# Two plain blocks in place of three at the start of channel mixers 2 to 4, with their gates behind the first seven-product block's products

## The chip, the cores and the metric

The kernel runs on one core of a Trainium2 chip, as one program. The time is the device's own time of one execution in microseconds (us); the median of several executions counts. TensorE is called PE, VectorE DVE, ScalarE ACT, GpSimd POOL and SyncE, which issues most of the DMAs, SP.

## The reference, cut to what matters

The program is a decoder trunk of two layers on 512 tokens of width 1024 in float32. Each layer has a channel mixer, a token mixer and a second channel mixer, and a last norm ends it. The change touches the channel mixers alone, of which there are four:

```python
def rmsnorm(x, g):
    y = x32 * lax.rsqrt(jnp.mean(x32 * x32, axis=-1, keepdims=True) + RMS_EPS)
    return y.astype(x.dtype) * g

def swiglu(x, w_gate, w_up, w_down):          # 1024 -> 2816 -> 1024
    return (jax.nn.silu(x @ w_gate) * (x @ w_up)) @ w_down

for i in range(2):
    h = h + 0.5 * swiglu(rmsnorm(h, ffn_norm_a[i]), ...)
    h = h + (mla_mixer, nsa_mixer)[i](...)
    h = h + 0.5 * swiglu(rmsnorm(h, ffn_norm_b[i]), ...)
return rmsnorm(h, final_norm)
```

## The kernel before, in words

The activations lie transposed, channels on the partitions and the 512 tokens along the free dimension, in eight tiles `h`. PE is given its operands as fp32r, and each operand is split into a high part (a copy by ACT) and a low part (the difference, by DVE), and each product is three matmuls: high by high, high by low, low by high. `split` does that; its two lines stand in the profile as L205 (ACT) and L206 (DVE). A weight slab is 128 x 1024 (all 1024 inputs of 128 outputs); `wslab` loads it by a DMA from SP and splits it (L176, L178).

`ffn(idx, ...)` is one channel mixer; `idx` 0 to 3 are mixers 1 to 4. Its 2816 hidden channels are 22 blocks `f` of 128. There are two kinds of block:

- A plain block multiplies a gate slab and an up slab by the activations (`plain`; tiles `pg` and `pu`, L401 to L403): 2 slabs x 8 inputs x 2 token halves x 3 = 96 matmuls of 256 columns.
- A seven-product block (`wsums` and `product`; tiles `px`, `pq`, `pg`, L386 to L388) computes the gate and up outputs of both token halves together, from sums of weights and sums of activations: 7 products x 4 inputs x 3 = 84 matmuls. DVE makes the weight sums (L372 to L376; `s1`, and in place in `rg` or `wr`, `ru`), ACT copies partial outputs out of PSUM (L543 to L550) and DVE adds the rest (L551, L553). The products come as 1, 7, 6, 2, 5, 4, 3. `w[1], w[2]` are halves of the slab's own split `w`; `w[7], w[4]` are `wh`/`wl` made from `ru`, `w[6], w[3]` those made from the sums in `rg` (or `wr`), `w[5]` those made from `s1`.

The activations' sums for these products are made by `combine(p)`, p = 0 to 3, once for each mixer: two scaled copies by ACT (`y`), three differences by DVE (`u`, L271 to L273), and a split of 1024 columns (`four`). A mixer therefore begins with plain blocks, `PLAIN = 3` of them, while the four combines are made; the other 19 are seven-product blocks.

The norm is applied late: `norm_col` finds 1/rms of each token (a chain of small DVE operations on `small`), `norm_bcast` spreads it by four PE transposes into a PSUM bank `pb`, and ACT copies it to a tile `row`. `gate(f, g)` multiplies the gate output by `row`, applies Silu (ACT, L434) and multiplies by `row` again (L433, L435); `act(f)` multiplies by the up output (L444, L446) and splits the result into `ah`, `al`. ACT must load its table of Silu once ahead of these where another function was used before; a one-element Silu on `tiny` (L513) sets its place.

The down projection runs in units: three blocks `f` (NG = 3) into one of eight output tiles, 9 matmuls of 512 columns (`pd`, L197 to L199), with a slab `wdr` from SP that is split into `wd`. The eight units of blocks 0 to 2 stand behind the seven-product blocks 3, 4 and 5, three, three and two of them. `settle` (the loop over `gates` on L525 to L527) lets ACT read one column of each plain gate bank, so that ACT is seen to be done with it.

A scheduler sets the order in each engine's queue from the program's text, its dependencies and a model of costs; each engine runs its queue in that order. `issue_after(x)` keeps an instruction behind x in that order. Two of them matter: the split of the slab of block `PLAIN + 1` is kept behind `evicted`, ACT's copy after product 5 of a block (here of block `PLAIN`), and the split of the down units of blocks 0 to 2 is kept behind the copy to `row` in mixers 2 and 4.

PSUM has eight banks in rings: `mm` 2, `S` 2, `T` 3, `o` 1. The gates of the plain blocks take all of `T`; the up outputs alternate between `mm` and `S`.

Of the kernel before, what the change touches and what calls it, by code (L numbers as in the profile page):

```python
# [11 lines left out]
F32 = mybir.dt.float32  # L12
F32R = mybir.dt.float32r
I32 = mybir.dt.int32
AF = mybir.ActivationFunctionType
# [33 lines left out]
PLAIN = 3  # L49
# [12 lines left out]
class Kern:  # L62
# [278 lines left out]
    def wsums(self, idx, f):  # L341
# [3 lines left out]
        if f == PLAIN:  # L345

            rg = fp.tile([P, 1024], F32, tag="fr", bufs=3, name="rg")
        else:
            rg = self.wp.tile([P, 1024], F32, tag="wr", bufs=2, name="wr")
# [6 lines left out]
        def split(src, pool, tag, bufs):  # L356
# [8 lines left out]
            with self.tc.issue_after(self.evicted.ins) if f == PLAIN + 1 else nullcontext():  # L365
                self.split(src, hi, lo)
# [57 lines left out]
    def ffn(self, idx, gain_next, ap, tp):  # L424
        nc, a = self.nc, self.a
        self.scr, self.fp = (tp, "sq", 1), tp
        ah, al, ht, row = {}, {}, [], None
        tg, tu, units = {}, {}, []
# [11 lines left out]
        def act(f):  # L440
            t = tu[f]
            if f < PLAIN:
                t = tu_tile()
                nc.vector.scalar_tensor_tensor(t, tu[f], -1.0, tg[f], op0=ALU.mult, op1=ALU.mult)  # L444
            else:
                nc.vector.tensor_tensor(t, t, tg[f], op=ALU.mult)  # L446
# [12 lines left out]
        def unit(tag, b0, c):  # L459
# [4 lines left out]
            with self.tc.issue_after(self.spread.ins) if idx % 2 and not b0 else nullcontext():  # L464
                self.split(raw.rearrange("p (k c) -> p k c", c=P), *w)
# [21 lines left out]
        gates = [self.bank("T", "pg") for _ in range(PLAIN)]  # L487
        for f, g in enumerate(gates):
# [23 lines left out]
            if f == 1:  # L512
                nc.scalar.activation(self.tiny[:, 4:5], col[:, 0:1], AF.Silu, scale=-1.0)  # L513
                pb = self.norm_bcast(col)
                row = tp.tile([P, S], F32, tag="row", bufs=1, name="row")
                self.spread = nc.scalar.activation(row, pb, AF.Copy)
                for e in range(2):
                    gate(e, gates[e])
                    act(e)
            elif f:  # L520
                gate(f, g)
                act(f)
            for p in (((0,), (1,), (2, 3)) if idx else ((0, 1), (2,), (3,)))[f]:
                self.combine(p)
        t = self.tiny  # L525
        for i, g in enumerate(gates[::-1]):
            nc.scalar.activation(t[:, i + 1 : i + 2], g[:, 0:1], AF.Identity, bias=t[:, i : i + 1])  # L527

        tail = PLAIN + (NF - 2 - PLAIN) // NG * NG
        for f in range(PLAIN, NF):  # L530
            if f % NG == 0 and f <= tail:
# [13 lines left out]
            nc.scalar.activation(uq[:, :HS], q, AF.Copy)  # L545
            self.product(6, w, x, False, False)
# [976 lines left out]
```

## Time and profile before

| | us |
|---|---|
| median of 3 runs | 1867.71 (1866.2 to 1868.5) |
| the profiled execution's own time | 1865.65 |
| its span, first to last instruction | 1863.9 |
| granted PE clock over the span | 0.999 |
| PE busy | 1849.9, 12448 matmuls |
| DVE, ACT, POOL busy | 1506.2, 1068.5, 297.4 |
| mixers 2, 3, 4: PE's first plain matmul | 546.45, 884.06, 1516.19 |

A row of the time line reads: start in us from the span's start, length in us, engine, line of the kernel, operation, output <- inputs, sizes, and, in brackets, how long the engine had been idle before it and what ended that. SPq is SP's queue of DMA issues. The lengths of PE's matmuls overlap, so their places are read from one start to the next.

### The profile page before, as it was taken

The numbers are of one execution on the slowest core, as the hardware profiler recorded it, in microseconds if no ns is written. First come the engines' busy times: TensorE is split into PE (matmuls) and PEld (weight loads), VectorE is DVE, ScalarE is ACT, GpSimd is POOL, SyncE is SP. The second block draws the span as 40 slices with busy tenths as digits, with TensorE's granted clock in tenths as the row PEclk, the third lists the DMA queues.
The fourth block names the chain that finished last, engine by engine and source line by source line (L and its number), as shares of the span: only waits on it lengthen the run. The fifth ranks groups of instructions, "written<-read, shape, count | busy, mean of one in ns | idle before, by whom it ended". The sixth has DMA issues, their size and how long they took to land.

```text
span 1863.9 us, 32992 instructions
## 1 busy us (share of the span) xinstructions
PE 1849.9 (99%) x12448; PEld 1686.5 (90%) x12448; DVE 1506.2 (81%) x2810; ACT 1068.5 (57%) x1997; POOL 297.4 (16%) x370
## 2 busy tenths in 40 slices
PE   9999999999999999999999999999999999999998
PEld 9999999878889999998999999988888889999997
DVE  8988886688779888886898887676878888888885
ACT  7555553577666555554655555445776865555554
POOL 0000000258830000001000000022666620000000
PEclk9999999999999999999999999999999999999999
DMA  6333331334433333322433332162433133333321
GB/s 238 125 114 102 102 91 47 117 103 105 115 124 112 116 102 104 112 74 64 142 120 110 107 107 80 44 180 84 108 109 103 41 118 122 114 104 105 104 78 69
DMA packets 84335, 196.38 MB, mean 105 GB/s; under 512 B 10944, under 2 KB 38464, under 8 KB 84176
## 3 DMA queue, kind: packets, MB, share of 16 engines
q1 hardware_dynamic: 81664, 191.34, 33.7%
q10 hardware_dynamic: 2512, 2.93, 0.5%
q8 instruction: 98, 1.61, 0.4%
q14 instruction: 61, 0.50, 0.1%
HBM read 178.44 MB, written 2.16 MB: 97 GB/s over the span
## 4 chain that ended last, share of the span: by engine, by line
PE 92%; DVE 3%; ACT 1%; issue 1%; POOL 1%; DMA 1%; SPq 0%; ACTq 0%; DVEq 0%; POOLq 0%
PE pd L198 8%; PE pd L197 8%; PE pd L199 8%; PE px L386 6%; PE px L388 5%; PE px L387 5%; PE pg L386 4%; PE pg L387 4%; PE pg L388 4%; PE pq L386 4%; PE pq L387 4%; PE pq L388 4%; PE o L1326 2%; PE pt L1299 2%; PE po L197 1%; PE po L199 1%
## 5 line engine op out<-in xcount | busy, mean ns | idle before, releaser
L198 PE MATMUL pd<-al,wd 128*128 128x512 f32 x576 | 225.1, 391 | 0.0
L197 PE MATMUL pd<-ah,wd 128*128 128x512 f32 x576 | 224.9, 390 | 0.0
L199 PE MATMUL pd<-ah,wd 128*128 128x512 f32 x576 | 224.6, 390 | 0.0
L289 POOL TENSOR_TENSOR s<-s,sq 128x512 f32<-128x512 f32 x38 | 54.9, 1445 | 1051.2 <-ACT sq L285 1051.2
L206 DVE TENSOR_TENSOR w<-wr,w 128x1024 fp32r<-128x1024 f32 x72 | 88.1, 1224 | 132.9 <-ACT w L205 132.6
L386 PE MATMUL px<-four,wh 128*128 128x256 f32 x608 | 168.4, 277 | 0.4 <-ACT pg L543 0.3
L388 PE MATMUL px<-four,wl 128*128 128x256 f32 x608 | 168.1, 277 | 0.2 <-DVE wl L206 0.2
L386 PE MATMUL pq<-four,wh 128*128 128x256 f32 x608 | 167.9, 276 | 0.0
L387 PE MATMUL px<-four,wh 128*128 128x256 f32 x608 | 167.9, 276 | 0.0
L388 PE MATMUL pq<-four,wl 128*128 128x256 f32 x608 | 167.8, 276 | 0.0
L387 PE MATMUL pq<-four,wh 128*128 128x256 f32 x608 | 167.8, 276 | 0.0
L457 DVE SCALAR_TENSOR_TENSOR h<-pd,h 128x512 f32<-128x512 f32 x216 | 147.5, 683 | 13.7 <-PE pd L199 13.6
L205 ACT ACTIVATE wd<-wdr 128x384 fp32r<-128x384 f32 x192 | 99.2, 519 | 98.5 <-ACT wd L205 58.2
L199 PEld LDWEIGHTS pd<-ah,wd 128*128 128x128 f32 x576 | 108.2, 188 | 22.7
L176 ACT ACTIVATE w<-wr 128x1024 fp32r<-128x1024 f32 (+3 forms) x89 | 80.8, 908 | 82.9 <-PE pd L199 19.2
L197 PEld LDWEIGHTS pd<-ah,wd 128*128 128x128 f32 x576 | 108.1, 188 | 20.5
L198 PEld LDWEIGHTS pd<-al,wd 128*128 128x128 f32 x576 | 108.1, 188 | 19.5
L178 DVE TENSOR_TENSOR w<-wr,w 128x1024 fp32r<-128x1024 f32 (+3 forms) x75 | 78.4, 1046 | 48.9 <-ACT w L176 48.7
L717 ACT ACTIVATE p<-p,small 128x512 f32<-128x512 f32 (+2 forms) x192 | 106.9, 558 | 19.1 <-DVE small L716 15.4
L386 PEld LDWEIGHTS px<-four,wh 128*128 128x128 f32 x608 | 114.1, 188 | 1.7 <-ACT pg L543 0.8
L388 PEld LDWEIGHTS px<-four,wl 128*128 128x128 f32 x608 | 114.1, 188 | 0.8 <-DVE wl L206 0.6
L386 PEld LDWEIGHTS pq<-four,wh 128*128 128x128 f32 x608 | 114.1, 188 | 0.4 <-ACT uq L545 0.4
(379 smaller groups left out, 6153.9 us busy)
## 6 DMA issues: line engine op xcount, KB each, us to landing
wr<-in_w_gu SPq DMA_DIRECT2D x93, 512.0 KB, 3.3
ru<-in_w_gu SPq DMA_DIRECT2D x76, 512.0 KB, 4.1
wdr<-in_w_down SPq DMA_DIRECT2D x192, 192.0 KB, 2.4
wr<-in_w_down SPq DMA_DIRECT2D x24, 256.0 KB, 2.6
wr<-in_mla_w_o SPq DMA_DIRECT2D x8, 512.0 KB, 3.6
th<-btab_d SPq DMA_DIRECT2D x16, 256.0 KB, 3.8
wr<-in_nsa_w_q SPq DMA_DIRECT2D x8, 512.0 KB, 3.9
wr<-in_nsa_w_o SPq DMA_DIRECT2D x8, 512.0 KB, 3.8
```

The source lines that it names most:

```text
L176: self.copied = nc.scalar.activation(wh[:, m], raw[:, m], AF.Copy)
L178: nc.vector.tensor_tensor(wl[:, m], raw[:, m], f32v(wh[:, m]), op=ALU.subtract)
L197: mm(out, wh, xh, start=first, stop=False)
L198: mm(out, wh, xl, start=False, stop=False)
L199: return mm(out, wl, xh, start=False, stop=last)
L205: nc.scalar.activation(hi, src, AF.Copy)
L206: (nc.gpsimd if pool else nc.vector).tensor_tensor(lo, src, f32v(hi), op=ALU.subtract)
L386: mm(out, wh[:, p], xh, start=first and p == 0, stop=False, skip_group_check=True)
L387: mm(out, wh[:, p], xl, start=False, stop=False, skip_group_check=True)
L388: mm(out, wl[:, p], xh, start=False, stop=last and p == KP - 1, skip_group_check=True)
L457: nc.vector.scalar_tensor_tensor(self.h[c], p, 0.5, self.h[c], op0=ALU.mult, op1=ALU.add)
L717: nc.scalar.activation(p_sb[:, :n], p_sb[:, :n], AF.Exp, bias=nm, scale=-1.0, accum_out=sm)
```

## The change

Mixer 1 keeps its three plain blocks. In mixers 2 to 4 block 2 becomes a seven-product block, the two plain blocks each make two combines ahead of it, and the copy to `row`, the gates and acts of blocks 0 and 1 and `settle` move behind products 1 and 7 of that block in the program's text. `PLAIN` becomes `self.plains`, 2 or 3. Block 2 has no down units behind it; those of blocks 0 to 2 stay behind blocks 3, 4 and 5, and their splits are kept behind `evicted` (of the block that they follow) in place of the copy to `row`. The split kept behind `evicted` is that of block 3, the second seven-product block.

```diff
@@ -46,7 +46,6 @@
 LASTK = 4
 HS = S // 2
 KP = KC // 2
-PLAIN = 3
 PAD = 16
 TILES = 24
 XC = P + 2
@@ -342,7 +341,7 @@
 
 
         nc, fp, w_gu = self.nc, self.fp, self.a["w_gu"]
-        if f == PLAIN:
+        if f == self.plains:
 
             rg = fp.tile([P, 1024], F32, tag="fr", bufs=3, name="rg")
         else:
@@ -362,7 +361,7 @@
             else:
                 hi = pool.tile([P, n], F32R, tag=tag[0], bufs=bufs, name="wh")
                 lo = pool.tile([P, n + 2 * PAD], F32R, tag=tag[1], bufs=bufs, name="wl")[:, 2 * PAD :]
-            with self.tc.issue_after(self.evicted.ins) if f == PLAIN + 1 else nullcontext():
+            with self.tc.issue_after(self.evicted.ins) if f == self.plains + 1 else nullcontext():
                 self.split(src, hi, lo)
             return [(hi[:, x : x + S].rearrange("p (k c) -> p k c", c=P), lo[:, x : x + S].rearrange("p (k c) -> p k c", c=P))
                     for x in range(0, n, S)]
@@ -425,6 +424,7 @@
         nc, a = self.nc, self.a
         self.scr, self.fp = (tp, "sq", 1), tp
         ah, al, ht, row = {}, {}, [], None
+        self.plains = 2 if idx else 3
         tg, tu, units = {}, {}, []
 
         def gate(f, g):
@@ -439,7 +439,7 @@
 
         def act(f):
             t = tu[f]
-            if f < PLAIN:
+            if f < self.plains:
                 t = tu_tile()
                 nc.vector.scalar_tensor_tensor(t, tu[f], -1.0, tg[f], op0=ALU.mult, op1=ALU.mult)
             else:
@@ -461,7 +461,7 @@
             w = [ap.tile([P, NG * P], F32R, tag=t, bufs=3, name="wd").rearrange("p (k c) -> p k c", c=P) for t in ("dh", "dl")]
             raw = ap.tile([P, NG * P], F32, tag="dr", bufs=2, name="wdr")
             nc.sync.dma_start(raw, a["w_down"][idx, c, :, b0 * P : (b0 + NG) * P])
-            with self.tc.issue_after(self.spread.ins) if idx % 2 and not b0 else nullcontext():
+            with self.tc.issue_after(self.evicted.ins) if idx and not b0 else nullcontext():
                 self.split(raw.rearrange("p (k c) -> p k c", c=P), *w)
             p = self.bank(tag, "pd")
             down(p, w, b0, b0 + NG)
@@ -484,7 +484,21 @@
             return self.norm_col(D, self.s2)
 
 
-        gates = [self.bank("T", "pg") for _ in range(PLAIN)]
+        def spread():
+            nonlocal row
+            pb = self.norm_bcast(col)
+            row = tp.tile([P, S], F32, tag="row", bufs=1, name="row")
+            nc.scalar.activation(row, pb, AF.Copy)
+            for e in range(2):
+                gate(e, gates[e])
+                act(e)
+
+        def settle():
+            t = self.tiny
+            for i, g in enumerate(gates[::-1]):
+                nc.scalar.activation(t[:, i + 1 : i + 2], g[:, 0:1], AF.Identity, bias=t[:, i : i + 1])
+
+        gates = [self.bank("T", "pg") for _ in range(self.plains)]
         for f, g in enumerate(gates):
             u = tu[f] = self.bank(("mm", "S")[f % 2], "pu")
             if idx == f == 0:
@@ -511,24 +525,19 @@
                 col = late()
             if f == 1:
                 nc.scalar.activation(self.tiny[:, 4:5], col[:, 0:1], AF.Silu, scale=-1.0)
-                pb = self.norm_bcast(col)
-                row = tp.tile([P, S], F32, tag="row", bufs=1, name="row")
-                self.spread = nc.scalar.activation(row, pb, AF.Copy)
-                for e in range(2):
-                    gate(e, gates[e])
-                    act(e)
-            elif f:
+            if f == 1 and idx == 0:
+                spread()
+            elif f > 1:
                 gate(f, g)
                 act(f)
-            for p in (((0,), (1,), (2, 3)) if idx else ((0, 1), (2,), (3,)))[f]:
+            for p in (((0, 1), (2, 3)) if idx else ((0, 1), (2,), (3,)))[f]:
                 self.combine(p)
-        t = self.tiny
-        for i, g in enumerate(gates[::-1]):
-            nc.scalar.activation(t[:, i + 1 : i + 2], g[:, 0:1], AF.Identity, bias=t[:, i : i + 1])
-
-        tail = PLAIN + (NF - 2 - PLAIN) // NG * NG
-        for f in range(PLAIN, NF):
-            if f % NG == 0 and f <= tail:
+        if idx == 0:
+            settle()
+
+        tail, left = (NF - 2) // NG * NG, 1
+        for f in range(self.plains, NF):
+            if f % NG == 0 and NG <= f <= tail:
                 units = [partial(unit, b0=f - NG, c=c) for c in range(KC)]
                 left = NG if f < tail else NF - tail
             n = -(-len(units) // left)
@@ -543,6 +552,9 @@
             nc.scalar.activation(g[:, :HS], x, AF.Copy)
             self.product(7, w, q, True, False)
             nc.scalar.activation(uq[:, :HS], q, AF.Copy)
+            if idx and f == self.plains:
+                spread()
+                settle()
             self.product(6, w, x, False, False)
             nc.scalar.activation(uq[:, HS:], x, AF.Copy)
             self.product(2, w, g[:, :HS], False, True)
```

What this does to the queues is shown at three places of mixer 2. In the names, the number tells tiles apart. Before, `rg_6834`, `w_6839`, `px_6858`, `pq_6859` belong to the first seven-product block (f = 3), `w_7018`, `px_7037`, `pq_7038` to the second (f = 4) and `w_7197` to the third. Now `rg_6686`, `px_6710`, `pq_6711` belong to the first (f = 2), `w_6848`, `px_6867`, `pq_6868` to the second (f = 3), and `w_7027`, `pq_7047` to the third (f = 4).

ACT, where the table load for Silu stands. Before:

```order
L176 ACTIVATE w_6697<-wr_6695 128x1024
L513 ACT_TABLE_LOAD
L513 ACTIVATE gains_77<-small_76 128x1
L176 ACTIVATE w_6750<-wr_6748 128x1024
L516 ACTIVATE row_6662<-pb_6657 128x512
```

Now:

```order
L204 ACTIVATE wh_6702<-rg_6686 128x1024
L527 ACT_TABLE_LOAD
L527 ACTIVATE gains_77<-small_76 128x1
L552 ACTIVATE pg_6712<-px_6710 128x256
L554 ACTIVATE uq_6713<-pq_6711 128x256
L491 ACTIVATE row_6746<-pb_6741 128x512
```

The load now stands between the split of the first seven-product block's weight sums and the copy of its product 1.

DVE, from the gates of blocks 0 and 1 on. Before:

```order
L433 TENSOR_TENSOR tg_6664<-pg_6406,row_6662 128x512
L433 TENSOR_TENSOR tg_6674<-pg_6407,row_6662 128x512
L206 TENSOR_TENSOR wd_6958<-wdr_6959,wd_6957 128x384
L435 TENSOR_TENSOR tg_6664<-tg_6664,row_6662 128x512
L435 TENSOR_TENSOR tg_6674<-tg_6674,row_6662 128x512
L444 SCALAR_TENSOR_TENSOR tu_6668<-pu_6409,tg_6664 128x512
L444 SCALAR_TENSOR_TENSOR tu_6678<-pu_6549,tg_6674 128x512
L433 TENSOR_TENSOR tg_6801<-pg_6408,row_6662 128x512
L206 TENSOR_TENSOR al_6671<-tu_6668,ah_6670 128x512
L206 TENSOR_TENSOR w_6839<-rg_6834,w_6839 128x1024
```

Now:

```order
L205 TENSOR_TENSOR wl_6703<-rg_6686,wh_6702 128x1024
L433 TENSOR_TENSOR tg_6748<-pg_6406,row_6746 128x512
L433 TENSOR_TENSOR tg_6758<-pg_6407,row_6746 128x512
L435 TENSOR_TENSOR tg_6748<-tg_6748,row_6746 128x512
L444 SCALAR_TENSOR_TENSOR tu_6752<-pu_6408,tg_6748 128x512
L435 TENSOR_TENSOR tg_6758<-tg_6758,row_6746 128x512
L205 TENSOR_TENSOR w_7027<-wr_7022,w_7027 128x1024
L205 TENSOR_TENSOR al_6755<-tu_6752,ah_6754 128x512
L444 SCALAR_TENSOR_TENSOR tu_6762<-pu_6558,tg_6758 128x512
L563 TENSOR_TENSOR tu_6714<-px_6710,uq_6713 128x256
L565 TENSOR_TENSOR tu_6714<-pq_6711,uq_6713 128x256
L205 TENSOR_TENSOR w_6848<-wr_6843,w_6848 128x1024
```

The gates stood ahead of the low half `w` of the first seven-product block; they now stand behind that block's low halves and ahead of the second block's, and the third block's `w_7027` stands ahead of the second's `w_6848`, as on ACT.

PE, where product 6 of the second seven-product block ends. Before:

```order
L386 MATMUL px_7037<-four_6828,wh_7029 128x256
L387 MATMUL px_7037<-four_6828,wh_7029 128x256
L388 MATMUL px_7037<-four_6828,wl_7030 128x256
L386 MATMUL pg_7039<-x_6263,w_7018 128x256
L387 MATMUL pg_7039<-x_6263,w_7018 128x256
```

Now:

```order
L385 MATMUL px_6867<-four_6683,wh_6859 128x256
L386 MATMUL px_6867<-four_6683,wh_6859 128x256
L387 MATMUL px_6867<-four_6683,wl_6860 128x256
L385 MATMUL pq_7047<-four_6545,wh_7032 128x256
L386 MATMUL pq_7047<-four_6545,wh_7032 128x256
L385 MATMUL px_6867<-four_6545,wh_6863 128x256
L386 MATMUL px_6867<-four_6545,wh_6863 128x256
```

Two matmuls of product 7 of the third block, whose weights `wh_7032` ACT makes from a sum on DVE, have moved ahead of product 5 of the second.

## The prediction

> **What bounds the kernel now.** I read the page first, then the busy time of each engine in stretches around the start of the second channel mixer, then the time line of each engine there.
>
> ```profile
> PE 1849.9 (99%) x12448; PEld 1686.5 (90%) x12448; DVE 1506.2 (81%) x2810; ACT 1068.5 (57%) x1997; POOL 297.4 (16%) x370
> PE 92%; DVE 3%; ACT 1%; issue 1%; POOL 1%; DMA 1%; SPq 0%; ACTq 0%; DVEq 0%; POOLq 0%
> ```
>
> PE carries 92% of the chain that ended last. A matmul taken away is worth its place in PE's row, as long as PE then finds its operands ready. The first and the last of the 48 matmuls of one slab of up-weights give that place:
>
> ```profile
> 551.94 0.28 PE L401 MATMUL pu<-x,w 128*128 128x256 f32 x1
> ...
> 557.27 0.28 PE L403 MATMUL pu<-x,w 128*128 128x256 f32 x1
> ```
>
> 47 steps in 5.33 us are 0.1134 us a matmul (the 0.28 us are its length; they overlap).
>
> The stretches below are of the second mixer: its first two plain blocks, the third, the first seven-product block, and the three down-projection units behind it. Columns: stretch, length, busy us of PE, weight loads, DVE, ACT, POOL, granted clock, DMA.
>
> ```profile
> 546.40:569.30 22.90, 22.90 (x200) 22.69 (x200) 21.45 (x37) 17.48 (x22) 3.29 (x2) 1.00 0.53 186
> 569.30:580.90 11.60, 11.55 (x102) 11.38 (x101) 10.29 (x18) 7.46 (x15) 0.00 (x0) 1.00 0.35 109
> 580.90:590.50 9.60, 9.60 (x84) 9.40 (x83) 6.70 (x10) 5.93 (x9) 0.00 (x0) 1.00 0.30 96
> 590.50:596.80 6.30, 6.30 (x31) 5.28 (x31) 6.30 (x11) 3.41 (x7) 0.00 (x0) 1.00 0.26 86
> ```
>
> This is where the argument turns. Over the kernel DVE is busy 81%, but in the two plain blocks 21.45 of 22.90 us, since the four sums for the seven products are made there. DVE is free for 1.45 + 1.31 + 2.90 = 5.66 us up to the end of the first seven-product block, and that is all the room.
>
> **What the change adds and removes.** Three mixers each turn one plain block (96 matmuls) into a seven-product one (84): 36 matmuls x 0.1134 = 4.1 us less on PE. DVE's prices, as starts from one row to the next:
>
> ```profile
> 555.19 1.22 DVE L206 TENSOR_TENSOR four<-u,four 128x1024 fp32r<-128x1024 f32 x1
> ...
> 558.40 0.42 DVE L273 TENSOR_TENSOR u<-y,u 128x256 f32<-128x256 f32 x1
> 558.74 0.42 DVE L272 TENSOR_TENSOR u<-y,u 128x256 f32<-128x256 f32 x1
> ...
> 561.14 0.15 DVE L294 TENSOR_SCALAR small<-pc 128x4 f32<-128x4 f32 x1
> 561.22 0.41 DVE L272 TENSOR_TENSOR u<-y,u 128x256 f32<-128x256 f32 x1
> ...
> 575.99 0.68 DVE L433 TENSOR_TENSOR tg<-pg,row 128x512 f32<-128x512 f32 x1
> 576.59 0.68 DVE L206 TENSOR_TENSOR al<-tu,ah 128x512 fp32r<-128x512 f32 x1
> 577.18 1.21 DVE L206 TENSOR_TENSOR w<-rg,w 128x1024 fp32r<-128x1024 f32 x1
> 578.32 0.68 DVE L206 TENSOR_TENSOR al<-tu,ah 128x512 fp32r<-128x512 f32 x1
> ...
> 588.11 1.23 DVE L206 TENSOR_TENSOR w<-wr,w 128x1024 fp32r<-128x1024 f32 x1 [2.83 <-ACT w L205]
> ```
>
> So 1.14 us for 1024 wide, 0.60 for 512, 0.34 for 256, some 0.08 to 0.10 for the norm's small ones; another engine sees a result 0.08 us after the next could start, and starts about 0.06 us later. A seven-product block costs DVE 3 x 1.14 + 0.60 (weights' low halves), 4 x 0.60 (weight sums), 2 x 0.34 (the outputs' sums), 4 x 0.60 (gate and act) = 9.5 us; a plain one 2 x 1.14 + 4 x 0.60 = 4.7. That is 4.8 us more for DVE, and 1.4 us less of PE to hide it, against 5.66 us of room: already 0.5 us short if nothing ever waits. The work that hid it is one plain block's PE time and the units behind the first seven-product block; now a second seven-product block follows the first with no units between.
>
> **First wait: product 6 of the new block, second mixer alone.** ACT must copy product 1 out of px before product 6 may add to it. In the order after, ACT's row ahead of that copy is: high half of rg, table load, the small Silu. Their prices:
>
> ```profile
> 566.66 1.05 ACT L176 ACTIVATE w<-wr 128x1024 fp32r<-128x1024 f32 x1
> 567.73 1.28 ACT L513 ACT_TABLE_LOAD   x1
> 569.53 0.20 ACT L513 ACTIVATE gains<-small 128x1 f32<-128x1 f32 x1 [0.52 <-DVE small L304]
> ...
> 570.77 0.60 ACT L516 ACTIVATE row<-pb 128x512 f32<-128x512 f32 x1
> ...
> 588.38 0.37 ACT L550 ACTIVATE pg<-px 128x256 f32<-128x256 f32 x1 [0.30 <-PE px L388]
> ```
>
> The table load stood beside a full PE before. The high half of rg needs the weight sums in rg, on DVE. From the row at 555.19 DVE has, up to that sum, 8 rows of 1.14, 5 of 0.60, 6 of 0.34 and 11 of 0.10 = 15.3, so 570.5. ACT then: 570.65 + 1.07 (from the row at 566.66 to the next) + 1.28 + 0.20 + a copy of 0.37 = 573.6. On PE's side:
>
> ```profile
> 569.32 0.28 PE L403 MATMUL pu<-x,w 128*128 128x256 f32 x1
> 569.65 0.62 PE L323 MATMUL pb<-ident,small 128*128 128x128 f32 x4
> 570.02 0.37 PE L401 MATMUL pg<-x,w 128*128 128x256 f32 x1
> ```
>
> PE ends the second plain block at 569.4, needs 24 x 0.1134 for products 1 and 7 and 0.37 + 0.11 for the transposes: 572.6. A wait of 1.0. In the third mixer the order has no table load there, in the fourth it stands earlier; between 0 and the second's 1.0 I take 0.2 and 0, nearest to "no load in the way".
>
> **Second wait: the second seven-product block.** DVE starts on the two moved gates when the norm's row is spread: 573.6 + 0.37 (copy of pq) + 0.60 = 574.5, 0.9 after product 6 began. From there to the sum that product 7 of the *third* seven-product block needs, DVE's order has 17 rows of 0.60, 4 of 1.14 and 2 of 0.34 = 15.4, and three short waits for ACT (Silu, the high half of w, 0.4 together): 590.3. With 0.14 to get there ACT splits that sum in 1.07, so PE may take the two matmuls on pq_7047 at 591.6. PE itself has between its product 6 at 573.6 and these two 120 matmuls (five products of the first block; 1, 2, 7, 4 and 6 of the second) = 13.6 us: it would be there at 587.2. The difference, 4.4 us, is PE's wait. It comes in pieces, by the same count up to each row: about 0.9 at the third matmul of product 1 (ACT may split w_6848 only behind its copy after product 5, and ahead of it ACT and DVE split a later block's w_7027; behind it on ACT stand wh_6853 for product 7 and the high half of act 1), 0.9 at product 2 (ACT's copy of px stands behind a Silu that waits for DVE), 0.75 at product 6, 1.1 at pq_7047, the rest small. In-order PE makes each of them whole: behind pq_7047 stands product 5, which is ready. Four shorter ones follow, up to the end of the third seven-product block (product 3, the low half of the first wd, product 6, the third unit), 0.05 to 0.1 each with 0.11 for the restart (next fence): 0.7. So 5.1 a mixer, 15.3 for three. The relation of row, gates and product 6 is the same in mixers 3 and 4, and so is the order from there on.
>
> The bounds of this term: at least 0.5 (the balance above, if every row were at its best place); at most DVE's 4.8 us and the whole 2.83 us idle of the row at 588.11 lost as well, 7.6.
>
> **What goes away.** Four waits of PE around the old first seven-product block:
>
> ```profile
> 583.86 0.28 PE L387 MATMUL px<-four,wh 128*128 128x256 f32 x1
> 584.13 0.39 PE L388 MATMUL px<-four,wl 128*128 128x256 f32 x1
> 584.36 0.28 PE L386 MATMUL px<-four,wh 128*128 128x256 f32 x1
> ...
> 615.42 0.28 PE L388 MATMUL pq<-four,wl 128*128 128x256 f32 x1
> 615.98 0.39 PE L386 MATMUL px<-four,wh 128*128 128x256 f32 x1 [0.28 <-ACT pg L543]
> ...
> 920.74 0.28 PE L388 MATMUL pq<-four,wl 128*128 128x256 f32 x1
> 921.12 0.38 PE L386 MATMUL px<-four,wh 128*128 128x256 f32 x1
> ...
> 1553.43 0.28 PE L387 MATMUL px<-four,wh 128*128 128x256 f32 x1
> 1553.94 0.39 PE L388 MATMUL px<-four,wl 128*128 128x256 f32 x1 [0.24 <-DVE wl L206]
> ```
>
> After a wait the next step is 0.23, as from 584.13 to 584.36, so each costs 0.11 beyond its own step less 0.1134: 0.27 + 0.56 + 0.37 + 0.51 = 1.7 us. I take all of it as gone, since the places are worked through anew above.
>
> **At nothing:** the third combine brought forward lies within DVE's 15.3 above; the one settle instruction less, and ACT's four copies and two splits more a mixer (ACT has 17.48 of 22.90 us busy, then 7.46 of 11.60; where it is late, it is because DVE is); the down units' splits behind product 5's copy in place of the norm's row, since PE wants them only after products 4 and 3, 2.7 us later; the DMAs, as many and as large as before. The third wdr lands later, since its buffer comes free only with the low half of the first; I count it in the 0.7 and price it below.
>
> **Sum, against the profiled execution (1865.65 us):** -4.1 - 1.7 + 15.3 + (1.0 + 0.11) + (0.2 + 0.11) = +10.9, so 1876.6. The median of the runs before, 1867.71, lies 2.06 higher; I forecast 1878.6 us for the median after.
>
> **The rivals.**
>
> *The matmuls' saving comes through (faster).* If ACT and DVE have the second block's weights ready, the time is 1867.7 - 4.1 = 1863.6. The place is the low half of w_6848; it turns to a gain where all waits of a mixer stay under (4.1 + 1.7) / 3 = 1.9 us. For it speaks PE's 99%; against it the four stretches. The Trainium skill, "Perfetto Trace Analysis", section "Identifying the Most-Contended Engine", tells one to speed up the engine with the highest occupancy first; by that rule the 36 matmuls are the whole story. The same page says that this engine can change over a kernel's course; here the stretches show DVE at 94% beside PE at 100%.
>
> *Half the waits.* If PE's operands come two or three rows earlier than I count (a scheduler's row that finds its buffer free sooner), 2.5 a mixer: +3, 1870.7. Against it: the same count on the rows of before.
>
> ```profile
> 571.92 1.28 DVE L433 TENSOR_TENSOR tg<-pg,row 128x512 f32<-128x512 f32 x2
> 573.12 0.55 DVE L206 TENSOR_TENSOR wd<-wdr,wd 128x384 fp32r<-128x384 f32 x1
> 573.59 1.28 DVE L435 TENSOR_TENSOR tg<-tg,row 128x512 f32<-128x512 f32 x2
> ...
> 582.87 1.21 DVE L206 TENSOR_TENSOR wl<-rg,wh 128x1024 fp32r<-128x1024 f32 x1
> ```
>
> Between the first and the last of these stand 14 rows of 0.60, three of 0.47 and one of 1.14, 10.95 us: 582.87, as the trace has it.
>
> *A late third wdr.* Its buffer comes free with the low half of the first wd, which the count puts at 596.1, and PE wants it at 600.
>
> ```profile
> wdr<-in_w_down SPq DMA_DIRECT2D x192, 192.0 KB, 2.4
> ```
>
> The last number is the median to landing. If it is late by 1.5 us in each mixer: 1883.1.
>
> *The clock falls.* Should PE lose half its clock in the waits, the 84 matmuls of one block a mixer cost 9.5 us more: 1907. The 0.56 us wait at 615 left no mark in the profile's clock row, and none of my waits is over 1.2. The Trainium skill, "TensorE: Matmul & The Clock Gate", section "HAM oscillation — how this bites in real kernels", names idle gaps of more than some 3.4 us as the limit; no run here shows such a gap.
>
> **How the numbers follow.** My forecast (4 to 6.5 us of waits a mixer) 0.70; half the waits 0.12; the late wdr 0.10; the saving in full 0.05; the clock 0.03. A measurement tells apart about 0.2%, 3.7 us; half the waits falls inside that. Faster 0.05, same 0.12, slower 0.83. The forecast's own range is 1874.5 to 1882.5; for 8 in 10 I widen it to the late wdr above and towards half the waits below: 1872.5 to 1884.
>
> **What the profile after would show.** PE 36 matmuls fewer; in the second mixer a gap before product 6 with ACT's table load beside it; in each of mixers 2 to 4 some 12 to 16 us behind that, waits of PE on w, pg and pq that add to 4 to 5 us while DVE has no idle; the units behind unchanged. I am wrong if DVE shows idle time in the second seven-product block, if ACT splits w_6848 before product 5 ends, or if PE's order does not bind there.

## The result and the profile after

The changed kernel takes 1878.23 us (median of 5 runs, 1877.28 to 1879.76); the kernel before 1866.66 us (5 runs, 1865.91 to 1868.5). The ratio is 1.0061, 95% interval 1.0050 to 1.0071: 0.6% slower. The profiled execution took 1877.28 us, with a span of 1875.5.

The page of the kernel after, busy time by engine and the chain by engine:

```profile
PE 1850.9 (99%) x12412; PEld 1685.1 (90%) x12412; DVE 1522.3 (81%) x2834; ACT 1076.0 (57%) x2012; POOL 295.8 (16%) x370
PE 91%; DVE 4%; ACT 1%; issue 1%; DMA 1%; POOL 1%; SPq 0%; ACTq 0%; POOLq 0%; DVEq 0%
```

PE has its 36 matmuls fewer and is as long busy as before: the lengths of matmuls overlap, and one behind a wait counts 0.38 us in place of 0.28, so short waits vanish in the busy time. The shares of the span say nothing of the loss. The same columns as before, for the second mixer's two plain blocks, its first seven-product block, its second, and the units:

```profile
547.20:570.00 22.80, 22.80 (x202) 22.77 (x201) 21.97 (x37) 16.25 (x21) 2.85 (x2) 1.00 0.52 186
570.00:581.30 11.30, 10.44 (x91) 10.19 (x91) 9.73 (x17) 9.32 (x17) 0.00 (x0) 1.00 0.13 46
581.30:594.50 13.20, 10.20 (x79) 9.29 (x77) 13.16 (x20) 7.03 (x13) 0.00 (x0) 1.00 0.25 82
594.50:600.80 6.30, 6.30 (x36) 5.42 (x35) 6.17 (x10) 2.98 (x6) 0.00 (x0) 1.00 0.60 179
```

In the third row the two engines have changed places: DVE works 13.16 of 13.20 us, PE 10.20. PE's waits in the whole kernel (engine, line, what for; us in total, times, longest) name them:

```profile
PE pq L385 <- ACT wh L204: 3.0, 3, 1.0
...
PE px L387 <- DVE w L205: 2.7, 3, 0.9
PE pg L385 <- ACT pg L552: 2.1, 3, 0.7
PE px L387 <- DVE wl L205: 1.2, 3, 0.4
...
PE px L385 <- ACT pg L552: 0.9, 1, 0.9
```

Four waits come three times, once in each changed mixer; the last row comes once, ahead of product 6 of the second mixer. PE's time line there (start, length, and in brackets the idle time with what ended it; start to start less 0.1134 is what a wait costs, and the step behind it, 0.22, costs 0.11 more):

```profile
572.67 0.60 PE L322 MATMUL pb<-ident,small 128*128 128x128 f32 x4
574.13 0.38 PE L385 MATMUL px<-four,wh 128*128 128x256 f32 x1 [0.86 <-ACT pg L552]
...
581.46 0.28 PE L386 MATMUL pq<-four,wh 128*128 128x256 f32 x1
582.63 0.39 PE L387 MATMUL px<-x,w 128*128 128x256 f32 x1 [0.89 <-DVE w L205]
...
583.80 0.28 PE L387 MATMUL px<-x,w 128*128 128x256 f32 x1
584.77 0.38 PE L385 MATMUL pg<-x,w 128*128 128x256 f32 x1 [0.69 <-ACT pg L552]
...
590.92 0.28 PE L387 MATMUL px<-four,wl 128*128 128x256 f32 x1
592.21 0.39 PE L385 MATMUL pq<-four,wh 128*128 128x256 f32 x1 [1.01 <-ACT wh L204]
```

DVE's time line beside it: the first gates, the third block's low half, the second block's, and the sum that ends the chain:

```profile
574.89 1.29 DVE L433 TENSOR_TENSOR tg<-pg,row 128x512 f32<-128x512 f32 x2 [1.34 <-ACT row L491]
...
578.35 1.23 DVE L205 TENSOR_TENSOR w<-wr,w 128x1024 fp32r<-128x1024 f32 x1
...
581.36 1.22 DVE L205 TENSOR_TENSOR w<-wr,w 128x1024 fp32r<-128x1024 f32 x1
...
590.37 0.69 DVE L372 TENSOR_TENSOR ru<-ru,wr 128x512 f32<-128x512 f32 x1
```

Between the first and the last of these the time line shows no idle time ahead of any row. ACT splits the second block's slab (w_6848) at 579.19, right behind its copy after product 5 of the first block at 578.88. So none of the three signs of being wrong came. And ACT, with the table load beside PE's gap ahead of product 6:

```profile
571.11 1.06 ACT L204 ACTIVATE wh<-rg 128x1024 fp32r<-128x1024 f32 x1 [3.74 <-DVE small L303]
572.19 1.28 ACT L527 ACT_TABLE_LOAD   x1
573.48 0.20 ACT L527 ACTIVATE gains<-small 128x1 f32<-128x1 f32 x1
573.71 0.37 ACT L552 ACTIVATE pg<-px 128x256 f32<-128x256 f32 x1
```

### The profile page after: what moved, and what is told of

Read it like the earlier page. It is cut to its first block, busy times and chain, and to the rows that moved or that the text cites. A ratio compares the mean times of both kernels' runs of the same rounds, so it can differ in the third digit from the quotient of the medians.

```text
span 1875.5 us, 32985 instructions
## 1 busy us (share of the span) xinstructions
PE 1850.9 (99%) x12412; PEld 1685.1 (90%) x12412; DVE 1522.3 (81%) x2834; ACT 1076.0 (57%) x2012; POOL 295.8 (16%) x370
## 4 chain that ended last, share of the span: by engine, by line
PE 91%; DVE 4%; ACT 1%; issue 1%; DMA 1%; POOL 1%; SPq 0%; ACTq 0%; POOLq 0%; DVEq 0%
PE pd L198 8%; PE pd L197 8%; PE pd L196 8%; PE px L385 6%; PE px L386 6%; PE px L387 6%; PE pg L385 4%; PE pg L386 4%; PE pg L387 4%; PE pq L385 4%; PE pq L387 4%; PE pq L386 4%; PE o L1338 2%; PE pt L1311 2%; PE po L196 1%; PE po L198 1%
## 5 line engine op out<-in xcount | busy, mean ns | idle before, releaser
L288 POOL TENSOR_TENSOR s<-s,sq 128x512 f32<-128x512 f32 x38 | 54.2, 1425 | 1060.2 <-ACT sq L284 1060.1
L385 PE MATMUL pq<-four,wh 128*128 128x256 f32 x632 | 175.0, 277 | 3.0 <-ACT wh L204 3.0
L385 PE MATMUL px<-four,wh 128*128 128x256 f32 x632 | 176.0, 278 | 0.9 <-ACT pg L552 0.9
L387 PE MATMUL px<-four,wl 128*128 128x256 f32 x632 | 175.0, 277 | 1.2 <-DVE wl L205 1.2
L386 PE MATMUL px<-four,wh 128*128 128x256 f32 x632 | 174.7, 276 | 0.0
L386 PE MATMUL pq<-four,wh 128*128 128x256 f32 x632 | 174.6, 276 | 0.0
L387 PE MATMUL pq<-four,wl 128*128 128x256 f32 x632 | 174.5, 276 | 0.0
L385 PEld LDWEIGHTS pq<-four,wh 128*128 128x128 f32 x632 | 118.6, 188 | 4.0 <-ACT wh L204 3.6
L175 ACT ACTIVATE w<-wr 128x1024 fp32r<-128x1024 f32 (+3 forms) x83 | 74.5, 898 | 81.0 <-PE pd L198 17.7
L385 PEld LDWEIGHTS px<-four,wh 128*128 128x128 f32 x632 | 118.6, 188 | 2.6 <-ACT pg L552 1.1
L387 PEld LDWEIGHTS px<-four,wl 128*128 128x128 f32 x632 | 118.6, 188 | 2.1 <-DVE wl L205 1.8
L386 PEld LDWEIGHTS px<-four,wh 128*128 128x128 f32 x632 | 118.6, 188 | 0.0
L386 PEld LDWEIGHTS pq<-four,wh 128*128 128x128 f32 x632 | 118.6, 188 | 0.0
```

What stands on the lines that cost most here:

```text
L175: self.copied = nc.scalar.activation(wh[:, m], raw[:, m], AF.Copy)
L288: nc.gpsimd.tensor_tensor(self.s2, self.s2, sq, op=ALU.add)
L385: mm(out, wh[:, p], xh, start=first and p == 0, stop=False, skip_group_check=True)
L386: mm(out, wh[:, p], xl, start=False, stop=False, skip_group_check=True)
L387: mm(out, wl[:, p], xh, start=False, stop=last and p == KP - 1, skip_group_check=True)
```

## The experiments

The table holds all eleven. Each ratio is against runs of the kernel before, taken in turn with it on the same chip. The two lengths are read from each profiled execution: from the start of a mixer's first plain matmul to the start of the last matmul of its down-projection, mixers 2 and 3 together (they follow one another) and mixer 4. The code between the mixers is the same everywhere, and it takes 202.15 to 204.56 us from mixer 1 to mixer 2 and 295.81 to 296.35 from mixer 3 to mixer 4; the lengths leave that out, and so tell more than the medians. Mixer 4 is the same code in after, I and J and takes 318.31 to 318.78 us, so a difference under some 0.5 us in one mixer says nothing. Each length is that of one execution.

| kernel | ratio (95%) | mixers 2+3, us | mixer 4, us |
|---|---|---|---|
| before | 1 | 673.90 | 314.99 |
| after | 1.0061 (1.0050 to 1.0071) | 680.85 | 318.47 |
| A: two DVE rows more | 1.0077 (1.0064 to 1.0089) | 682.97 | 321.18 |
| B: two DVE rows left out | 1.0038 (1.0025 to 1.0051) | 678.68 | 317.49 |
| C: six DVE rows left out | 1.0017 (1.0008 to 1.0025) | 676.61 | 316.76 |
| D: two DVE rows on POOL | 1.0056 (1.0043 to 1.0068) | 680.95 | 318.33 |
| E: gates where they were | 1.0050 (1.0038 to 1.0063) | 680.25 | 318.72 |
| F: third block's split later | 1.0074 (1.0061 to 1.0086) | 682.47 | 319.99 |
| G: PE's order held | 1.0069 (1.0055 to 1.0082) | 681.17 | 319.42 |
| H: C and G together | 1.0033 (1.0021 to 1.0046) | 677.30 | 316.91 |
| I: table load a block earlier | 1.0058 (1.0044 to 1.0071) | 682.61 | 318.31 |
| J: table load in ACT's gap | 1.0049 (1.0035 to 1.0062) | 679.97 | 318.78 |
| K: before, four DVE rows more | 1.0027 (1.0016 to 1.0038) | 676.62 | 316.90 |

After loses 6.95 + 3.48 us, some 3.5 in each changed mixer. In A (mixer 4) and I (mixer 3) 1.6 us of the length is the clock, told at the end.

**A, B and C: is it DVE's chain?** A computes the low halves of acts 0 and 1 twice:

```diff
             self.split(t, ah[f], al[f])
+            if idx and f < 2:
+                nc.vector.tensor_tensor(al[f], t, f32v(ah[f]), op=ALU.subtract)
```

> The low halves of acts 0 and 1 are computed twice by DVE in mixers 2 to 4, two more rows of 0.60 us behind the row, one ahead of the low half of the second block's weights and one right behind it. Theory (the second block's waits are DVE's unbroken chain of rows from the gates on): 1.2 us more a mixer, 3.6 us more than after in all, 0.6 of each at the third matmul of product 1. Rival (ACT's copies and high halves, or the order of PE, set the waits): 0 to 0.5 us more. Rival (the chain has slack at its end): 0.6 a mixer, 1.8 us.

Measured: 2.12 us more in mixers 2 and 3, so 1.06 each, and 2.71 - 1.6 = 1.1 in mixer 4. The first rival falls; the second's 0.6 does as well. One detail missed: the third matmul of product 1 waits no longer than in after (a start-to-start gap of 1.11 us for 1.17), since the two sums of the first block's output moved behind that low half; the added time comes at products 7, 4 and 6 instead.

B leaves the same rows out, with no other engine in their place:

```diff
+            if idx and f < 2:
+                nc.scalar.activation(ah[f], t, AF.Copy)
+                al[f] = ah[f]
+                return
```

> Left out: the low halves of acts 0 and 1 in mixers 2 to 4 (the high half is used in their place), so two DVE rows of 0.60 us behind the row are gone, without POOL beside them; the orders of DVE and ACT are after's apart from that. Theory (DVE's unbroken chain sets the second block's waits, and the run with POOL failed because POOL's rows took 1.8 to 2.0 us, held up the output's sum by 0.6 and stretched a DVE row by 0.5): 1.2 us less a mixer, 3.6 us less than after. Rival (DVE is not what the waits hang on; the orders of PE and ACT are): 0 within 1, as with POOL.

Measured: 2.17 us less in mixers 2 and 3, 0.98 in mixer 4, so 1.05 a mixer for 1.2 us of rows. In both directions PE pays nine tenths of what DVE's rows take.

C leaves out six rows (the condition is f <= 2, and further:)

```diff
-            nc.vector.tensor_tensor(t, t, row, op=ALU.mult)
+            if not idx or f > 1:
+                nc.vector.tensor_tensor(t, t, row, op=ALU.mult)
...
+            if idx and f == self.plains + 1 and n == S:
+                with self.tc.issue_after(self.evicted.ins):
+                    nc.scalar.activation(hi, src, AF.Copy)
+                lo = hi
...
```

> Left out in mixers 2 to 4: six DVE rows of 0.60 us ahead of the third block's sum: the low halves of acts 0, 1 and 2 and of the second block's sum s1 (the high halves are used in their place) and the second multiplication of gates 0 and 1 by the row. Theory (DVE's chain): up to 3.6 us less a mixer, 10.8 less than after, that is the time of before again; 8 to 10.8 if ACT's rows end last at some of the places. Rival (PE's order, with the third block's two matmuls in the second block, or ACT): the wait at the third block's pq of 1.2 us and half of the others stay, at most 5 us less.

Measured: 4.24 us less in mixers 2 and 3 and 1.71 in mixer 4, 2.0 a mixer and 5.95 in all, between the theory's 8 and the rival's 5. The whole kernel's ratios don't settle it: they differ by 0.0044, some 8 us, but by their intervals this can be 5.7 to 10.7 (an estimate). From the first gate to the same sum DVE takes 11.75 us, where after took 15.48. The six rows are gone, and one of 1.14 has moved behind the sum; but DVE, which had no idle time there in after, now waits 1.08 us for ACT:

```profile
575.46 1.29 DVE L438 TENSOR_TENSOR tg<-pg,row 128x512 f32<-128x512 f32 x2 [1.34 <-ACT row L501]
...
579.41 1.23 DVE L205 TENSOR_TENSOR w<-wr,w 128x1024 fp32r<-128x1024 f32 x1 [1.08 <-ACT w L204]
...
587.21 0.69 DVE L377 TENSOR_TENSOR ru<-ru,wr 128x512 f32<-128x512 f32 x1
```

The wait at the third block's pq is gone, but others end last now. PE and ACT of C, where product 1 ends and product 2 begins:

```profile
583.63 0.28 PE L392 MATMUL px<-x,w 128*128 128x256 f32 x1
584.37 0.38 PE L390 MATMUL pg<-x,w 128*128 128x256 f32 x1 [0.46 <-ACT pg L562]
```

```profile
583.95 0.37 ACT L562 ACTIVATE pg<-px 128x256 f32<-128x256 f32 x1 [0.24 <-PE px L392]
```

ACT was idle and waited for PE here: 0.74 us from the last matmul of product 1 to the first of product 2 is the bare way over ACT's copy, and no faster DVE shortens it. In after the same place took 0.97, of which only 0.23 was DVE's.

**D: the same two rows on POOL.** `self.split(t, ah[f], al[f], pool=bool(idx) and f < 2)`

> The same two rows (low halves of acts 0 and 1, mixers 2 to 4) are done by POOL, which is idle there; ACT's order is the same as in after, DVE's is after's without the two rows. Theory (DVE's chain): 1.2 us less a mixer, 3.6 us less than after in all. It may be less, 2.0, if ACT's rows end last once DVE is 0.6 earlier at a place. Rival (not DVE): 0. Rival (POOL slows DVE's rows beside it): more than after, and DVE's 128x512 rows over 0.68 us.

Measured: 0.1 us more in mixers 2 and 3, 0.1 less in mixer 4. Taken alone this would have spoken for "not DVE"; B showed that it doesn't. The time lines of POOL and of DVE in D:

```profile
579.15 1.83 POOL L205 TENSOR_TENSOR al<-tu,ah 128x512 fp32r<-128x512 f32 x1 [24.95 <-ACT ah L204]
582.02 2.04 POOL L205 TENSOR_TENSOR al<-tu,ah 128x512 fp32r<-128x512 f32 x1 [1.04 <-ACT ah L204]
```

```profile
578.59 1.23 DVE L205 TENSOR_TENSOR w<-wr,w 128x1024 fp32r<-128x1024 f32 x1
...
581.01 0.42 DVE L563 TENSOR_TENSOR tu<-px,uq 128x256 f32<-128x256 f32 x1 [0.60 <-POOL al L205]
...
581.69 1.21 DVE L205 TENSOR_TENSOR w<-wr,w 128x1024 fp32r<-128x1024 f32 x1
...
583.42 1.72 DVE L205 TENSOR_TENSOR wl<-ru,wh 128x1024 fp32r<-128x1024 f32 x1
```

The output's sum writes into a buffer that is free only when POOL has read act 0's t, so DVE waits 0.60 us for the slower engine; and a row of 1.22 that begins while POOL's second row runs takes 1.72. (The two rows of that size that were under way when POOL's began kept 1.23 and 1.21.) That gives back 1.1 of the 1.2 us.

**E: which part of the change?** Two plain blocks stay, the gates return to their place:

```diff
-            if f == 1 and idx == 0:
+            if f == 1:
                 spread()
...
-        if idx == 0:
-            settle()
+        settle()
...
-            if idx and f == self.plains:
-                spread()
-                settle()
```

> Two plain blocks in place of three stay, but row, gates and acts 0 and 1 are issued behind the plain blocks, ahead of the first seven-product block, as before: the change without its second part. Theory (the third plain block's 10.9 us of PE beside 4.7 us of DVE is what is missing; DVE has the same rows in the same stretch): within 1.5 us of after. Rival (the gates' place behind products 1 and 7 makes the waits): most of the 10 us come back.

Measured: 0.6 us less in mixers 2 and 3, 0.25 more in mixer 4. Where the gates stand is worth nothing that these runs can tell. What is left of the change is the missing plain block, with what comes with it: two combines in each plain block, and the places of the splits that are kept behind product 5's copy. No run takes these apart.

**F and G: is it an order?** F holds the third block's weight halves behind product 5's copy too:

```diff
-            with self.tc.issue_after(self.evicted.ins) if f == self.plains + 1 else nullcontext():
+            with self.tc.issue_after(self.evicted.ins) if f == self.plains + 1 or (idx and f == self.plains + 2) else nullcontext():
```

> In mixers 2 to 4 the third seven-product block's weight halves are also put behind product 5's copy of the block ahead, so ACT and DVE no longer split a later block's weights (1.14 us on DVE) ahead of the second block's, and PE's two matmuls of the third block in the middle of the second go back behind the units. Theory (DVE's chain, with the row of 1.14 in it): the first wait shrinks by 0.5, those at products 2 and 6 by 1.1 together, the one at pq of the third block (1.17 + 0.11) is gone, and the work put off finds room beside the units: 2 to 3 us less a mixer, 6 to 9 us less than after. Rival (the total of DVE's rows counts, not their order): the waits come back in the third block, 0 us within 1.

Measured: 1.6 us *more* in mixers 2 and 3 together and 1.5 in mixer 4, against a theory of 6 to 9 less. The first wait did shrink (a gap of 0.69 for 1.17 in the second mixer) and the one at the third block's pq went, but the matmuls that had filled PE's time there went with it: products 6, 5 and 3 now follow one another, each behind ACT's copy of the one ahead. PE's waits in F, over the three mixers:

```profile
PE pg L385 <- ACT pg L562: 2.1, 4, 0.7
PE px L385 <- ACT uq L559: 1.4, 3, 0.5
PE px L387 <- DVE w L205: 1.4, 3, 0.5
PE pg L385 <- ACT pg L552: 1.4, 3, 0.5
```

and new gaps of 0.25 to 0.70 from start to start stand in the third block. Putting w_7027 back behind w_6848 gains nothing by itself. What the hold on w_6848 itself costs (its place behind product 5's copy, as in before) no run tests.

G leaves that split where it is and holds PE's order (products 6 and 2 behind 7, nothing of the third block in the second):

```diff
+            def behind(last, d):
+                return self.tc.issue_after(last.ins) if idx and f == self.plains + d else nullcontext()
...
+            with behind(end, 1):
+                self.product(6, w, x, False, False)
...
+            with behind(self.end, 2):
+                self.product(1, w, x, True, False)
```

> In mixers 2 to 4 PE's order is held: the second seven-product block's products 6 and 2 come behind product 7, and no matmul of the third block comes into the second. Seen so far: with six DVE rows left out some 2.4 us of waits stay in the second block, each at a place where PE's order puts a product right behind the one whose copy it needs. Theory (in after DVE's chain ends last, so the waits only change place): 0 to 1 us less a mixer, 0 to 3 less than after. Rival (PE's order alone makes half of the waits): 2 us less a mixer, 6 less than after.

Measured: 0.3 us more in mixers 2 and 3 together and 0.95 in mixer 4. The rival falls, and the theory's sign is missed by a little: the waits change place, and PE's filling is lost.

H does C and G at once.

> Both at once: the six DVE rows a mixer left out (low halves of acts 0, 1, 2 and of s1, the second multiplication of gates 0 and 1 by the row; the high halves stand in) and PE's order held as in the run with the order alone. Theory (DVE's chain first, PE's order behind it: the order counts only once DVE is ahead): 1.0 to 1.5 us a mixer less than with the rows left out alone, that is 3 to 4.5 less than its 1871.5, at the time of before. Rival (the floor of 2.4 us is ACT's copies, whatever PE's order): 0 to 1 less than 1871.5.

Measured: 0.7 us *more* than C in mixers 2 and 3 together, and 0.15 in mixer 4. My theory fell: nothing was won, by the lengths or by the ratios. The rival's 0 to 1 less was missed too, by little more than these lengths can tell, and its mechanism is seen: holding the order makes the way over ACT's copies count more, since products 6, 5 and 3 stand end to end. PE's waits in H:

```profile
PE px L390 <- ACT uq L575: 1.4, 3, 0.5
PE pg L390 <- ACT pg L579: 1.4, 3, 0.5
```

Six waits of some 0.47 us, the size of the bare way in C.

**I and J: the table load.** I issues it a plain block earlier, on a constant:

```diff
+            if idx == 1 and f == 0:
+                with self.tc.issue_after(self.high.ins):
+                    nc.scalar.activation(self.tiny[:, 4:5], self.gains[:, 0:1], AF.Silu, scale=-1.0)
...
-            if f == 1:
+            if f == 1 and idx != 1:
```

> In the second mixer the table load (with the small Silu) is issued on a constant a plain block earlier, so ACT has it behind it long before product 6. Theory (the table load makes product 6 wait, and DVE starts on the gates only when the row that ACT copies behind the load is there): the wait of 1.08 + 0.11 us ahead of product 6 is gone, DVE's 1.34 us idle ahead of its first gate too, and the second block's waits stay as they are, since both engines come earlier by the same time: 1.2 us less than after, ratio to after 0.9994. Rival (DVE is the only bound, so that what ACT gains is lost again in the second block): 0 less, and the second block's waits grow by 1.2 us.

Measured: nothing won; without the clock's 1.6 us mixers 2 and 3 take 0.2 more. In the second mixer alone, the only one that was changed, it is 0.56 more up to the start of block 8. ACT and DVE of I:

```profile
551.00 1.28 ACT L506 ACT_TABLE_LOAD   x1
```

```profile
555.39 1.60 DVE L371 TENSOR_TENSOR s<-ru 128x512 f32<-128x512 f32 x1 [3.10 <-POOL s L288]
```

The load now stands ahead of rows that DVE needs for its sums. DVE's order changed too: the weight sum `s` moved ahead of the differences `u` and waits for POOL, DVE is idle for 3.10 us, and rg's high half, hence product 6, is as late as before: the wait there is 1.08 + 0.11 us again, though no load stands near, and 0.59 + 0.11 two matmuls on. The number is the rival's, but its sign isn't there: the second block's waits did not grow by 1.2, they are after's. Nothing came earlier, so neither was tested; the place was badly chosen. J puts the load behind the high half of the first block's rg, in the 3.74 us that ACT was idle:

```diff
         w[1], w[2] = split(rg, self.wp, None, 2)
+        if idx == 1 and f == self.plains:
+            with self.tc.issue_after(self.split_ins):
+                nc.scalar.activation(self.tiny[:, 4:5], self.gains[:, 0:1], AF.Silu, scale=-1.0)
...
-            if f == 1:
+            if f == 1 and idx != 1:
```

> In the second mixer the table load comes on a constant right behind the high half of the first block's rg, where ACT was idle for 3.74 us waiting for DVE; DVE's order is after's. In the run that moved it a plain block earlier it stood ahead of the row that DVE waited for, and DVE was idle there for 3.10 us. Theory: product 6's wait of 1.08 + 0.11 us goes and DVE starts on its gates 1.2 us earlier: 1.2 us less in the second mixer, none in the others. Rival (DVE would not be ready earlier anyway): 0.

Measured: 0.88 us less in mixers 2 and 3 (0.92 in the second, up to the start of block 8), 0.3 more in mixer 4, where nothing was changed. ACT, DVE and PE of J at product 6:

```profile
567.18 1.28 ACT L373 ACT_TABLE_LOAD   x1
...
572.00 0.37 ACT L555 ACTIVATE pg<-px 128x256 f32<-128x256 f32 x1
```

```profile
573.75 1.29 DVE L436 TENSOR_TENSOR tg<-pg,row 128x512 f32<-128x512 f32 x2 [0.39 <-ACT row L494]
```

```profile
572.84 0.37 PE L388 MATMUL px<-four,wh 128*128 128x256 f32 x1
573.04 0.28 PE L389 MATMUL px<-four,wh 128*128 128x256 f32 x1
573.41 0.39 PE L390 MATMUL px<-four,wl 128*128 128x256 f32 x1
```

The wait of 1.1 us ahead of product 6 is gone, 0.25 comes back two matmuls later, and DVE starts 1.0 us earlier than in after, counted from the mixer's start (573.75 - 547.04 for 574.89 - 547.22). So the load did cost about what the prediction said, 0.9 us for 1.0 + 0.11, though the ratio alone would not tell it from after.

**K: how much room was there before?** In the kernel before, the low halves of acts 0 and 1 are computed three times (the row of A, in a loop of two):

> The kernel before, with the low halves of acts 0 and 1 of mixers 2 to 4 computed three times: four DVE rows of 0.60 us more a mixer, in the stretch of the third plain block and the first seven-product block, where DVE was free for 1.31 + 2.90 us. Theory (that room is what the change uses up): at most 1 us more than before in all. Rival (DVE was at its limit in before already): 2.4 a mixer, 7.2 more.

Measured: 2.72 us more in mixers 2 and 3 and 1.91 in mixer 4. Up to the start of block 8 it is 0.47 us more in the second mixer, 2.24 in the third and 1.90 in the fourth, for 2.4 us of rows each. Both sizes fall. PE's waits in K:

```profile
PE pg L386 <- ACT pg L552: 1.2, 2, 0.6
...
PE px L386 <- ACT pg L545: 0.7, 1, 0.7
PE px L386 <- ACT wh L205: 0.7, 2, 0.3
```

Before's own list has a single row at that line:

```profile
PE px L386 <- ACT pg L543: 0.3, 1, 0.3
```

K has more than four rows added: the scheduler also changed the order of all three engines in the first seven-product block (in the second mixer PE's product 2 comes ahead of product 6). So it shows that the rows are not free, and not how much room there was. Where DVE's 5.66 us lay can be read in before's own rows. Of the third plain block's 1.31 us, 1.28 stand ahead of this row, when the norm's row was not yet spread (ACT copies it at 570.77):

```profile
570.78 1.23 DVE L178 TENSOR_TENSOR w<-wr,w 128x1024 fp32r<-128x1024 f32 x1 [1.28 <-ACT w L176]
```

Of the first seven-product block's 2.90 us, 2.83 stand ahead of the row at 588.11 (shown in the prediction), behind the low half at 582.87 that PE's matmul at 584.13 waits for. Between the gates at 571.92 and that low half DVE is never idle: in the chain that matters there was no room.

No kernel here is faster than before: all eleven ratios are above 1.

## Why the prediction was right, point by point

- *36 matmuls, 4.1 us:* 12448 to 12412 matmuls, at the same step. As said.
- *The four old waits, 1.7 us:* none is left at its place.
- *Product 6 of the second mixer, 1.0 + 0.11:* 1.08 + 0.11, with the load beside it; J took it away. The 573.6 for the copy was 573.71. In the third mixer 0.09 for 0.2 + 0.11, in the fourth two of 0.1 for nothing.
- *Second block, 5.1 a mixer:* in the second mixer the gaps beyond 0.1134 are 1.17 at product 1's third matmul (0.9 predicted), 0.96 at product 2 (0.9), 0.18 + 0.68 at product 6 (0.75), 1.28 at the third block's pq (1.1) and 0.4 in short ones (0.7 in four): 4.7, and the same within 0.05 in mixers 3 and 4. At product 2 the size is luck: the prediction put it down to a Silu that waits for DVE, but only 0.23 us is that, and 0.74 the bare way over ACT's copy, which C shows. DVE's chain was to run from 574.5 to 590.3; it ran from 574.89 to 590.97.
- *The sum:* -4.1 - 1.7 + 14.1 + 1.5 = 9.8, where 10.9 was predicted. The mixers' lengths give 10.4, the span 11.6: 0.6 in delays under 0.1 that I don't list, and 1.2 outside the changed mixers, in code that is the same. That the median came within 0.4 us of the forecast is therefore luck in part: the second block came out 1.2 us lower in the sum, and about as much was added outside.
- *Half the waits, the saving in full, the late wdr:* none came. Ahead of the units behind the second block PE doesn't wait at all, where the late wdr wanted 1.5.

Two steps were wrong without changing the number. The balance that gave 5.66 us of room, and from it a lower bound of 0.5 for the waits, counted DVE's idle time wherever it lay; before's rows show that 4.11 us of it lay ahead of the gates or behind the row that PE was waiting for, and none in the chain between, so the bound said little. And the waits were put down almost wholly to DVE's rows: A and B bear that out for the first 1.2 us either way (0.9 us of PE for 1 us of rows), and in C some 2.0 of the 4.7 go with six rows. In C's second mixer 2.4 us stay, from start to start 0.73 and 0.52 behind ACT's copies, 0.56 behind a low half of DVE, and the rest in steps of 0.17 to 0.29 behind ACT. Whether more DVE rows less would take any of that is not tested. The forecast held since, at after's own load, DVE is the one that ends last at every large wait of the second block but product 2, at the third block's pq by way of ACT's split.

The Trainium skill's rule ("Perfetto Trace Analysis", section "Identifying the Most-Contended Engine") points at PE by the whole kernel's occupancy, 99% before and after, and by the busy share of the weight loads, one of the two measures that it asks for with TensorE, 90% before and after; the four stretches, with DVE at 13.16 of 13.20 us, carried the sign.

## What to carry to other kernels

A block that is taken out also takes its cover away: before trading PE's work for another engine's, add up that engine's rows from the last free moment to the row that PE waits for, and set them against PE's time to that place; idle time behind that row is no room. Test such a count in both directions, a little more work and a little less, and take the work away rather than to a slower engine, whose own length and buffers can hide the answer. A table load cost nothing here only in ACT's own gap: look for a row with idle time ahead of it, not for "earlier". And see whether the scheduler has changed more than you did, as in K, before you read a price from a run.

## What the runs showed of the hardware that was not expected

The granted clock fell without a long gap. In I, third mixer, in windows of 3.5 us (PE's busy time first, the clock behind POOL's column):

```profile
923.70:927.20 3.50, 1.93 (x15) 1.53 (x13) 3.50 (x5) 1.90 (x4) 0.00 (x0) 1.00 0.02 5
927.20:930.70 3.50, 3.45 (x17) 3.45 (x17) 3.21 (x6) 0.41 (x3) 0.00 (x0) 0.53 0.47 150
```

After two waits (gaps of 1.17 and 1.00 us) 16 matmuls came every 0.213 us in place of 0.1134, 1.6 us in all, and then the step was as before. A shows the same once, in mixer 4, behind gaps of 1.04 and 1.29 us. After has the same two waits in all three mixers and G one of 1.55 in each, both without such a stretch, so the size of the waits alone doesn't decide it. The Trainium skill, "TensorE: Matmul & The Clock Gate", section "HAM oscillation — how this bites in real kernels", names gaps of more than some 3.4 us; here the longest ahead of such a stretch was 1.29. The same page, section "What's actually happening", tells of a free-running window of 3413 ns, which would fit both the length of the slow stretch and its coming in one execution and not in another; the runs don't show the window itself.

In D the rows of POOL and DVE held each other up, and the one that began second was the one that grew. POOL's two rows of 128x512 took 1.83 and 2.04 us, where a row of that size in L288 of after takes 1.35 in the median (1.29 to 1.81). The two 128x1024 DVE rows that were under way when these began kept 1.23 and 1.21 us; the one that began while POOL's second row ran took 1.72. It is the same for these three DVE rows, within 0.01 us, in mixers 3 and 4. The two 128x512 DVE rows beside POOL's with one input in PSUM kept their 0.68. The Trainium skill, "GPSIMD Engine Reference", section "8. Key points", says that POOL contends with VectorE's instructions that have two SBUF inputs; D agrees, since the rows that grew are POOL's and one such row of DVE.
